# Head loads in smaller pieces, and three bursts of small products per half of a gated recurrence

## The chip, the cores and the metric

The kernel runs on one core of one Trainium2 chip. The metric is the device time of one execution in microseconds (us); the median of several executions is compared. Engines are called PE (TensorE's products; PEld is its weight load), DVE (VectorE), ACT (ScalarE), POOL (GpSimd) and SP (SyncE, which here only issues transfers). PSUM is the memory that PE writes, in banks of 512 f32 per partition; the other tiles lie in SBUF, 128 partitions wide.

## What is computed

One layer of a decoder trunk on 256 tokens of 2048 features, all in f32. Cut to what matters here:

```python
h = rmsnorm(x, norm_mix_g)
u = h @ w_in                     # 2048 -> 12288, split into ten fields
c_g, b_g, xa, za, q, fl, iv, og, ga, gb = split(u)
ya = b_g * causal_dwconv3(c_g * xa, conv_w) * silu(za)
o  = hgrn2_chunked(silu(q), kk(fl), iv, log_f(fl))   # 8 heads of 128
yb = rmsnorm_per_head(o) * silu(og)
m  = sigmoid(ga) * (ya @ w_a_out) + sigmoid(gb) * (yb @ w_b_out)
x  = x + m @ w_o
x  = x + sigmoid(rmsnorm(x) @ w_ple_gate) * (p @ w_ple_proj)
return rmsnorm(x, final_norm_g)
```

The recurrence is a gated linear one: with b the running sum of log_f over the tokens,

```python
a[t, s] = sum_k q[t, k] * exp(b[t, k] - b[s, k]) * kk[s, k]   for s <= t
o[t]    = sum_s a[t, s] * v[s]
```

## The kernel before

**Big products.** Every f32 matrix is split into a high and a low part (`whi`, `wlo` for weights, `xh`, `xl` and the like for activations), and a product is the sum of high x high, high x low and low x high. The main loop at line 940 walks 292 steps. One step holds a chunk of 256 rows and 512 columns of a weight matrix: 2 k tiles x 2 token tiles x 3 parts = 12 products of 128x128 by 128x512 (line 937, in `product`). The groups follow in the order PP (p @ w_ple_proj, one step for each of four column groups), then the fields of w_in for j = 0 and j = 1 (f, q, iv, og, c, xa, za, b; eight steps each), then ga and gb with A and B, then O and PG. Weights come through `load` on SP's queue in tiles called `raw`, and `split` (line 113) makes `whi` on ACT (line 124) and `wlo` on DVE (line 125), three steps ahead of PE, in four buffers. p lies in `praw` and is split by `put_p` on DVE (lines 889 and 890); its split tiles share memory with those of ya and appear in the profile as `yaTh` and `yaTl`.

**The head.** `praw` is loaded in one transfer on SP (line 154). The first step's weights, 128 partitions x 1024, come in two transfers of 128 x 512 by `load_first(0, ...)` (line 106): columns 0 to 511, which are k tile 0, on ACT's queue and the rest on SP's. The second step's weights follow on SP, then small parameters, weights and x by turns. Meanwhile ten products of a zeroed tile (`WARM`, line 816) run on PE. At step 0 the first k tile's products come in the order high x high, low x high (of the activation), high x low.

**Epilogues.** Each group's results are worked on by a generator. `advance` lets each active generator go on to its next `yield` once a step, so that work is spread over steps beside the big products; `step` puts what a generator issues behind the newest split on ACT and DVE. The Tile framework orders the instructions of an engine and sets the semaphores.

**The recurrence.** `hgrn(j)` (line 351) handles four heads and 256 tokens (two blocks of 128) for each half j. Scores inside a block are made in levels B = 128, 64, 32, 16, 8, 4: a pair of tokens belongs to the level at which they lie in the two halves of one stretch of B tokens. `level(B)` (line 424) makes factors exp(+-(b - reference)) on DVE, POOL and ACT and multiplies them into kT and qT, giving a tile X; `products` (line 385) multiplies X's key part by its query part in small tiles (32 or 64 columns) into a PSUM bank; `keep` (line 394) copies the wanted entries under an integer mask into `both` (line 396, in pieces of 32 or 64 partitions). Pairs of neighbouring tokens (B = 2) are done with kT and qT scaled by `f` and `rf` (lines 488 to 501). The cross block between the two blocks of 128 tokens has its own X (line 481) and product (line 512). Two operations split `both` into the scores `a` of the two blocks (line 502), because the second block runs backwards. f32 products of this kind are two records each in the profile.

Before the change PE gets five bursts for each half: levels 128 and 64; 32 and 16; 8 and 4 (line 389, each level into a bank of its own); the cross block with the pairs (lines 512 and 389); and the scores times the values v (lines 529 to 531). Ahead of the last one DVE copies the cross block to `aoff` (line 522) and keeps the pairs by eight masked copies (line 524, recorded at 396).

**The tail.** `last_norm(t)` (line 756) scales the last result by a per-token factor r, in pieces on DVE and ACT, and stores each piece. It is called for t = 0 beside PE's last products, and for t = 1 at the very end.

Of the kernel before, what the change touches and what calls it, by code (L numbers as in the profile page):

```python
# [11 lines left out]
AF = mybir.ActivationFunctionType  # L12
ALU = mybir.AluOpType
PSUM = bass.MemoryType.PSUM

P = 128
T = 256
# [6 lines left out]
CW = 512  # L24
PLE = 256
EPS = 1e-6
WARM = 10
LB_FLOOR = 1e-30
LB_MAX = 1.0 - 1e-6
SCAN = 64  # L30
LEVELS = [128, 64, 32, 16, 8, 4]
# [13 lines left out]
def hybrid_kernel(ctx, tc, xT, x, pT, prm, gfin, masks, w_in, w_a, w_b, w_o, w_pg, w_pp, out):  # L45
    nc = tc.nc
# [35 lines left out]
    def bank(tag):  # L82
        return ps.tile([P, CW], F32, tag=tag, bufs=4, name=nm(tag))
# [22 lines left out]
    def load_first(pos, queues):  # L106

        w, g, c = stream[pos]
        n = 2 * CW // len(queues)
        for i, eng in enumerate(queues):  # L110
            eng.dma_start(out=load(pos)[:, pos % 2, i * n : (i + 1) * n], in_=w[g, :, c, i * n : (i + 1) * n])
# [239 lines left out]
    def hgrn(j):  # L351
# [33 lines left out]
        def products(bk, key, query, B):  # L385

            for h in range(4):
                for r, c in quarters(B):
                    nc.tensor.matmul(  # L389
                        heads(bk)[r, h, c], key(h)[:, r], query(h)[:, c], start=True, stop=True,  # L390
                        tile_position=(0, r.start),
                    )

        def keep(dst, mask, src, B):
            for r, c in quarters(B):
                nc.vector.copy_predicated(  # L396
                    out=dst[r, :, c], data=src[r, :, c],
                    mask=mask_t[r, mask : mask + 1, c].to_broadcast([r.stop - r.start, 4, c.stop - c.start]),
                )

        def halves(ap, B):
            r = ap.rearrange("p (n two h) -> p n two h", two=2, h=B // 2)
# [21 lines left out]
        def level(B):  # L424

            n, h = 1024 // B, B // 2
            e = t4()
            bl, br = halves(b, B)
            el, er = halves(e, B)
            if B > SCAN:  # L430
                nc.scalar.activation(out=el, in_=halves(y, B)[0], func=AF.Exp, scale=-1.0)
                nc.scalar.activation(out=er, in_=br, func=AF.Exp)
            else:
                ref = bl[:, :, h - 1 : h].to_broadcast([P, n, h])
                nc.vector.tensor_tensor(out=el, in0=bl, in1=ref, op=ALU.subtract)
# [9 lines left out]
            in1=tot.rearrange("p (n o) -> p n o", o=1).to_broadcast([P, 16, SCAN]), op=ALU.subtract,  # L445
        )
        yield
        Xs = [level(LEVELS[0])]
        yield
        yield  # L450
        Xs.append(level(LEVELS[1]))
        yield
        yield
        yield

        for i in range(0, len(LEVELS), 2):
            bks = [bank("s") for _ in range(2)]
            for n, X in enumerate(Xs):
                products(bks[n], lambda h: X[:, 0, h, :], lambda h: X[:, 1, h, :], LEVELS[i + n])
            more = i + 2 < len(LEVELS)  # L460
            Xs = [level(LEVELS[i + 2])] if more else []
            yield
            yield
            for n, bk in enumerate(bks):
                keep(both, i + n, heads(bk), LEVELS[i + n])
            if more:
                Xs.append(level(LEVELS[i + 3]))
                yield
                yield
                yield  # L470

        e = t4()
        el, er = halves(e, P)
# [2 lines left out]
            out=el, in0=yl,  # L476
# [4 lines left out]
        X = new_X()  # L481
# [25 lines left out]
        yield  # L507
        bo = bank("s")
        for h in range(4):
            for r in range(2):  # L510
                rows = slice(r * 64, (r + 1) * 64)
                nc.tensor.matmul(
                    heads(bo)[rows, h, :], X[:, 0, h, rows], X[:, 1, h, :], start=True, stop=True,
                    tile_position=(0, r * 64),
                )
# [6 lines left out]
        nc.vector.tensor_copy(out=aoff.rearrange("p h t -> p (h t)"), in_=bo)  # L522
# [233 lines left out]
    def last_norm(t):  # L756

        xs, r, tot = state["x"], sc(1, "r3", 2), state["tot3", t]
        nc.vector.tensor_tensor(out=tot, in0=tot, in1=state["ss3"][:, t * 6 + 4 : t * 6 + 5], op=ALU.add)
        nc.gpsimd.tensor_tensor(out=r, in0=tot, in1=mhalf[:, :1], op=ALU.pow)  # L760
        n = CW // 2

        for eng, q0, q1, queue in (
            (nc.vector, 4, 5, nc.sync), (nc.vector, 5, 6, nc.sync), (nc.scalar, 0, 2, nc.sync),
            (nc.vector, 6, 8, nc.sync), (nc.scalar, 2, 4, nc.scalar),
        ):
            s = slice(q0 * n, q1 * n)
            d = xs[:, t, s]
            if q0 >= 6:
# [3 lines left out]
            elif eng is nc.scalar:  # L773
                nc.scalar.activation(out=d, in_=d, func=AF.Identity, scale=r)
            else:
                nc.vector.tensor_scalar(out=d, in0=d, scalar1=r, scalar2=None, op0=ALU.mult)
            queue.dma_start(out=out[:, t, s], in_=d)

    def ep_last(t, halves):

# [335 lines left out]
```

## Time and profile before

| | |
|---|---|
| median of 3 executions | 831.42 us (831.42 to 831.85) |
| the profiled execution's own time | 831.84 us |
| its span, first to last instruction | 830.1 us |
| instructions in the span | 10589 |
| granted PE clock, mean | 0.996 |
| moved by DMA | 187.25 MB, mean 226 GB/s |

The profile shows one execution. Times in its rows are counted from the span's start. A row of a timeline gives start, length, engine, line, operation and tiles (out<-in), the number of merged instructions (x), and in brackets the idle time of the engine before it and what ended it. A row of a group gives busy us and mean ns of one, then idle time before it. The chain is the sequence of work that ended last, followed back from the last instruction. PE's products are pipelined: their recorded lengths overlap, and the pace is read from their starts.

### The profile page before, as it was taken

What the parts mean: (1) busy time and instruction counts of PE and PEld (TensorE: products, weight loads), DVE (VectorE), ACT (ScalarE), POOL (GpSimd) and SP (SyncE); (2) the same over time, 40 slices, a digit from 0 to 9 for tenths busy, and PEclk for the clock granted to TensorE, in tenths of its full rate; (3) what the DMA queues carried; (4) which work ended last, traced back from release to release, by engine and by line L of the source; (5) the groups of instructions that cost most, each with busy time, mean ns of one, the idle gap of its engine ahead of it and who ended that gap; (6) DMA issues with size and microseconds to landing.
All of it is one profiled execution on the core that took longest, in us unless ns stands there. A gap on an engine that the chain in (4) does not pass through costs nothing.

```text
span 830.1 us, 10589 instructions
## 1 busy us (share of the span) xinstructions
PE 816.9 (98%) x4122; PEld 674.3 (81%) x4122; DVE 538.3 (65%) x662; ACT 430.9 (52%) x553; POOL 84.8 (10%) x74
## 2 busy tenths in 40 slices
PE   9999999999999999999999999999999999999995
PEld 6888888878888888878888888888888888888885
DVE  6746678896866588896745545545645656679633
ACT  7666565446564465455544443443444455566522
POOL 1000035110000054100001001000100000001210
PEclk9999999999999999999999999999999999999998
DMA  9969655647876554657655755755655787987702
GB/s 341 372 256 340 222 193 197 204 153 219 277 235 232 203 203 152 204 192 241 227 203 172 254 189 196 253 203 191 231 191 198 253 281 246 330 304 269 293 0 103
DMA packets 40947, 187.25 MB, mean 226 GB/s; under 512 B 4672, under 2 KB 14400, under 8 KB 22720
## 3 DMA queue, kind: packets, MB, share of 16 engines
q1 hardware_dynamic: 40464, 185.78, 64.7%
q10 hardware_dynamic: 432, 0.79, 0.3%
q8 instruction: 32, 0.52, 0.3%
q14 instruction: 19, 0.16, 0.1%
HBM read 172.92 MB, written 13.63 MB: 225 GB/s over the span
## 4 chain that ended last, share of the span: by engine, by line
PE 93%; DVE 3%; issue 2%; ACT 1%; POOLq 0%; POOL 0%; DVEq 0%
PE g L937 91%; DVE wlo L125 1%; PE s L389 1%; PE s L937 1%; PE s L817 1%; DVE t L264 0%; PE s L531 0%; PE s L529 0%; DVE a L396 0%; ACT whi L124 0%; DVE both L396 0%; DVE X L483 0%; PE s L530 0%; DVE t L492 0%; DVE t L494 0%
## 5 line engine op out<-in xcount | busy, mean ns | idle before, releaser
L125 DVE TENSOR_TENSOR wlo<-raw,whi 128x1024 fp32r<-128x1024 f32 (+1 forms) x293 | 360.4, 1235 | 251.8 <-ACT whi L124 250.8
L124 ACT ACTIVATE whi<-raw 128x1024 fp32r<-128x1024 f32 (+1 forms) x293 | 307.6, 1056 | 323.6 <-PE g L937 279.4
L937 PE MATMUL g<-whi,xh 128*128 128x512 f32 (+1 forms) x912 | 352.0, 387 | 0.0
L937 PE MATMUL g<-whi,xl 128*128 128x512 f32 (+1 forms) x912 | 351.8, 386 | 0.0
L937 PE MATMUL g<-wlo,xh 128*128 128x512 f32 (+1 forms) x912 | 351.7, 386 | 0.0
L937 PEld LDWEIGHTS g<-whi,xh 128*128 128x128 f32 x912 | 171.3, 188 | 34.6
L937 PEld LDWEIGHTS g<-whi,xl 128*128 128x128 f32 x912 | 171.3, 188 | 34.3
L937 PEld LDWEIGHTS g<-wlo,xh 128*128 128x128 f32 x912 | 171.4, 188 | 33.9
L937 PE MATMUL g<-whi,mh 128*128 128x512 f32 x128 | 49.8, 390 | 0.0
L937 PE MATMUL g<-wlo,mh 128*128 128x512 f32 x128 | 49.7, 389 | 0.0
L937 PE MATMUL g<-whi,ml 128*128 128x512 f32 x128 | 49.6, 390 | 0.0
L659 POOL TENSOR_TENSOR t<-ga,gb 128x512 f32<-128x512 f32 x6 | 10.6, 1786 | 195.8 <-DVE gb L654 195.8
L937 PE MATMUL g<-whi,yaTh 128*128 128x512 f32 x72 | 28.3, 399 | 0.0
L937 PEld LDWEIGHTS g<-whi,mh 128*128 128x128 f32 x128 | 24.0, 188 | 5.3 <-ACT mh L665 0.3
L937 PE MATMUL g<-whi,yaTl 128*128 128x512 f32 x72 | 28.3, 396 | 0.0
L937 PEld LDWEIGHTS g<-whi,ml 128*128 128x128 f32 x128 | 23.9, 188 | 5.1 <-DVE ml L666 0.2
L937 PEld LDWEIGHTS g<-wlo,mh 128*128 128x128 f32 x128 | 24.0, 188 | 5.0
L937 PE MATMUL g<-wlo,yaTh 128*128 128x512 f32 x72 | 27.9, 390 | 0.0
L436 POOL TENSOR_TENSOR t<-b 128x512 f32<-128x512 f32 x10 | 18.9, 1890 | 67.0 <-DVE b L319 38.7
L937 PE MATMUL g<-whi,ybTh 128*128 128x512 f32 x64 | 24.9, 389 | 0.0
L937 PE MATMUL g<-whi,ybTl 128*128 128x512 f32 x64 | 24.9, 389 | 0.0
L937 PE MATMUL g<-wlo,ybTh 128*128 128x512 f32 x64 | 24.9, 389 | 0.0
(154 smaller groups left out, 522.4 us busy)
## 6 DMA issues: line engine op xcount, KB each, us to landing
raw<-in_w_in SPq DMA_DIRECT2D x93, 1024.0 KB, 5.0
raw<-in_w_o SPq DMA_DIRECT2D x16, 1024.0 KB, 5.5
raw<-in_w_pg SPq DMA_DIRECT2D x16, 1024.0 KB, 5.8
turn<-t SPq DMA_DIRECT2D x72, 128.0 KB, 2.7
t<-turn SPq DMA_DIRECT2D x18, 512.0 KB, 4.9
raw<-in_w_a SPq DMA_DIRECT2D x8, 1024.0 KB, 5.0
raw<-in_w_b SPq DMA_DIRECT2D x8, 1024.0 KB, 5.0
raw<-in_w_in SPq DMA_DIRECT2D x6, 512.0 KB, 8.3
```

The lines of the kernel that those rows point to most:

```text
L124: a = nc.scalar.activation(out=hi[:, s], in_=src[:, s], func=AF.Copy)
L125: v = nc.vector.tensor_tensor(out=lo[:, s], in0=src[:, s], in1=hi[:, s].bitcast(F32), op=ALU.subtract)
L389: nc.tensor.matmul(heads(bk)[r, h, c], key(h)[:, r], query(h)[:, c], start=True, stop=True, tile_position=(0, r.start),)
L436: nc.gpsimd.tensor_tensor(out=er, in0=br, in1=ref, op=ALU.subtract)
L659: (nc.vector if j == 3 else nc.gpsimd).tensor_tensor(out=spread(m, t), in0=blocks(ga[:, s]), in1=blocks(gb[:, s]), op=ALU.add)
L817: nc.tensor.matmul(wb, warm[:, :P], warm, start=True, stop=True)
L937: nc.tensor.matmul(psum, a, b, start=first and n == 0, stop=last and n == 2)
```

## The change

Four edits stand in the diff.

1. The head: p comes in two transfers (one per k tile) on SP. The first step's weights come, for each k tile, as partitions 0 to 63 on ACT's queue and 64 to 127 on SP's. Six warm-up products instead of ten.
2. The recurrence: the levels 32, 16, 8 and 4 are made first and multiplied in one burst into one bank (each level's 32-wide results at column 32 i of each head), and kept by four masked copies of a whole bank, whose source is repeated along the columns. The levels 128 and 64 are made afterwards and multiplied together with the cross block and the pairs, all in tiles of 32 columns: levels 128, 64 and the first block's pairs share a bank. They are kept by three whole-bank copies under combined masks, which DVE makes once at j = 0. `aoff` is copied by ACT, and one more `yield` stands between these copies and the last burst. Counting `yield`s from the recurrence's start, the bursts stand at 6, 11, 16, 22 and 25 before, at 11, 20 and 24 after.
3. Cross-block products in four tiles of 32 columns instead of two of 64.
4. The tail: `last_norm` uses four pieces of 512 columns instead of two of 256 and three of 512.

```diff
-WARM = 10
+WARM = 6
...
-    nc.sync.dma_start(out=praw.rearrange("p (k t) -> p k t", k=2), in_=pT)
-    load_first(0, (nc.scalar, nc.sync))
+    w0 = load(0)
+    for k in range(2):
+        s = slice(k * CW, (k + 1) * CW)
+        nc.sync.dma_start(out=praw[:, k * T : (k + 1) * T], in_=pT[:, k, :])
+        for eng, part in ((nc.scalar, slice(0, 64)), (nc.sync, slice(64, P))):
+            eng.dma_start(out=w0[part, 0, s], in_=w_pp[0, part, 0, s])
...
         def quarters(B):
-            n = max(B // 2, 32)
-            for r in range(P // n):
-                c = r ^ 1 if B >= 64 else r
-                yield slice(r * n, (r + 1) * n), slice(c * n, (c + 1) * n)
+            for r in range(0, P, 32):
+                c = {128: (r // 64 ^ 1) * 64, 64: r ^ 32}.get(B, r)
+                n = max(B // 2, 32)
+                yield slice(r, r + 32), slice(c, c + n)
...
-        def keep(dst, mask, src, B):
-            for r, c in quarters(B):
+        def keep(dst, mask, src, at=None):
+            if at is None:
                 nc.vector.copy_predicated(
-                    out=dst[r, :, c], data=src[r, :, c],
-                    mask=mask_t[r, mask : mask + 1, c].to_broadcast([r.stop - r.start, 4, c.stop - c.start]),
+                    out=dst, data=src, mask=mask_t[:, mask : mask + 1, :].to_broadcast([P, 4, P])
                 )
+                return
+            n = P // 32
+            nc.vector.copy_predicated(
+                out=dst.rearrange("p h (n c) -> p h n c", n=n),
+                data=src[:, :, at : at + 32].rearrange("p h (n c) -> p h n c", n=1).to_broadcast([P, 4, n, 32]),
+                mask=mask_t[:, mask : mask + 1, :].rearrange("p h (n c) -> p h n c", n=n).to_broadcast([P, 4, n, 32]),
+            )
...
-        Xs = [level(LEVELS[0])]
-        yield
-        yield
-        Xs.append(level(LEVELS[1]))
-        yield
-        yield
-        yield
-        for i in range(0, len(LEVELS), 2):
-            bks = [bank("s") for _ in range(2)]
-            for n, X in enumerate(Xs):
-                products(bks[n], lambda h: X[:, 0, h, :], lambda h: X[:, 1, h, :], LEVELS[i + n])
-            more = i + 2 < len(LEVELS)
-            Xs = [level(LEVELS[i + 2])] if more else []
+        if j == 0:
+            m = lambda i: mask_t[:, i, :]
+            for out, a0, a1, op in ((0, 0, 1, ALU.max), (1, 0, 7, ALU.mult), (0, 0, 6, ALU.mult), (0, 0, 8, ALU.max)):
+                nc.vector.tensor_tensor(out=m(out), in0=m(a0), in1=m(a1), op=op)
+        Xs = []
+        for i in range(2, len(LEVELS)):
+            Xs.append(level(LEVELS[i]))
             yield
             yield
-            for n, bk in enumerate(bks):
-                keep(both, i + n, heads(bk), LEVELS[i + n])
-            if more:
-                Xs.append(level(LEVELS[i + 3]))
+            if i % 2:
                 yield
-                yield
-                yield
+        bk = bank("s")
+        for i, X in enumerate(Xs):
+            products(bk, lambda h: X[:, 0, h, :], lambda h: X[:, 1, h, :], LEVELS[2 + i], 32 * i)
+        Xs = [level(LEVELS[0])]
+        yield
+        yield
+        for i in range(4):
+            keep(both, 2 + i, heads(bk), 32 * i)
+        Xs.append(level(LEVELS[1]))
+        yield
+        yield
+        yield
...
         bk = [bank("s") for _ in range(2)]
+        for i, X in enumerate(Xs):
+            products(bk[0], lambda h: X[:, 0, h, :], lambda h: X[:, 1, h, :], LEVELS[i])
         for blk in range(2):
             kk, qq = (z.rearrange("p (h k t) -> p h k t", h=4, k=2)[:, :, blk, :] for z in (kT, qT))
-            products(bk[blk], lambda h: kk[:, h, :], lambda h: qq[:, h, :], 2)
-        yield
-        yield
-        nc.vector.tensor_copy(out=aoff.rearrange("p h t -> p (h t)"), in_=bo)
-        for blk in range(2):
-            keep(a[:, blk], len(LEVELS) + 2 + blk, heads(bk[blk]), 2)
+            products(bk[blk], lambda h: kk[:, h, :], lambda h: qq[:, h, :], 2, 0 if blk else None)
+        yield
+        yield
+        nc.scalar.activation(out=aoff.rearrange("p h t -> p (h t)"), in_=bo, func=AF.Copy)
+        keep(a[:, 0], 0, heads(bk[0]))
+        keep(a[:, 1], 1, heads(bk[0]))
+        keep(a[:, 1], len(LEVELS) + 3, heads(bk[1]), 0)
+        yield
         yield
...
-        for eng, q0, q1, queue in (
-            (nc.vector, 4, 5, nc.sync), (nc.vector, 5, 6, nc.sync), (nc.scalar, 0, 2, nc.sync),
-            (nc.vector, 6, 8, nc.sync), (nc.scalar, 2, 4, nc.scalar),
-        ):
+        for q in (2, 0, 3, 1):
```

More of the change, by code (lines that the diff above doesn't have):

```diff
@@ L509, in hgrn @@
         for h in range(4):
[L510 to L511 removed]
+            for r in range(0, P, 32):
                 nc.tensor.matmul(
[L513 to L514 removed]
+                    heads(bo)[r : r + 32, h, :], X[:, 0, h, r : r + 32], X[:, 1, h, :], start=True, stop=True,
+                    tile_position=(0, r),
                 )
         bk = [bank("s") for _ in range(2)]
+        for i, X in enumerate(Xs):
+            products(bk[0], lambda h: X[:, 0, h, :], lambda h: X[:, 1, h, :], LEVELS[i])
         for blk in range(2):
             kk, qq = (z.rearrange("p (h k t) -> p h k t", h=4, k=2)[:, :, blk, :] for z in (kT, qT))
[L519 removed]
+            products(bk[blk], lambda h: kk[:, h, :], lambda h: qq[:, h, :], 2, 0 if blk else None)
         yield
         yield
[L522 to L524 removed]
+        nc.scalar.activation(out=aoff.rearrange("p h t -> p (h t)"), in_=bo, func=AF.Copy)
[3 more added lines that the diff above has]
+        yield
         yield
@@ L760, in last_norm @@
         nc.gpsimd.tensor_tensor(out=r, in0=tot, in1=mhalf[:, :1], op=ALU.pow)
-        n = CW // 2
-        for eng, q0, q1, queue in (
-            (nc.vector, 4, 5, nc.sync), (nc.vector, 5, 6, nc.sync), (nc.scalar, 0, 2, nc.sync),
-            (nc.vector, 6, 8, nc.sync), (nc.scalar, 2, 4, nc.scalar),
-        ):
-            s = slice(q0 * n, q1 * n)
-            d = xs[:, t, s]
-            if q0 >= 6:
+        for q in (2, 0, 3, 1):
+            s = slice(q * CW, (q + 1) * CW)
+            d = xs[:, t, s]
+            if q < 2:
+                nc.scalar.activation(out=d, in_=d, func=AF.Identity, scale=r)
+            elif q == 2:
+                nc.vector.tensor_scalar(out=d, in0=d, scalar1=r, scalar2=None, op0=ALU.mult)
+            else:
                 nc.vector.scalar_tensor_tensor(
@@ L772, in last_norm @@
                 )
[L773 to L777, printed above, removed]
+            (nc.scalar if q == 1 else nc.sync).dma_start(out=out[:, t, s], in_=d)
     def ep_last(t, halves):
```

6 lines of the change are left out of this document (3 added, 3 removed).

## The prediction

> **What bounds the kernel now.** I read the page first: the busy times, the busy row of TensorE (PE), the shares of the chain.
>
> ```profile
> PE 816.9 (98%) x4122; PEld 674.3 (81%) x4122; DVE 538.3 (65%) x662; ACT 430.9 (52%) x553; POOL 84.8 (10%) x74
> PE   9999999999999999999999999999999999999995
> PE 93%; DVE 3%; issue 2%; ACT 1%; POOLq 0%; POOL 0%; DVEq 0%
> ```
>
> PE is the bound from the first microseconds to the last slice. So an edit can gain only where PE does something other than its big products at their own pace: the head, the small products of the recurrence, the tail. The list of the chain's pieces in order of time shows the second of these, here for the first half (j = 0):
>
> ```profile
> 17.36 106.08 PE g L937 x468
> 123.44 1.00 PE s L389 x48
> 124.44 13.81 PE g L937 x60
> 138.25 0.69 PE s L389 x50
> 138.94 13.85 PE g L937 x60
> ...
> 170.05 1.02 PE s L512 x16
> 171.07 0.69 PE s L389 x50
> ```
>
> A big product takes 106.08 / 468 = 0.227 us, so one step of the main loop (12 products) takes 2.72 us. Sixty products would take 13.60, but the pieces between bursts take 13.81: each burst costs 0.21 us of switching beside its own time. The first four bursts thus cost 1.00 + 0.21 = 1.21, 0.90, 0.90 (the third, at 152.79, has the piece of the second) and 1.02 + 0.69 + 0.21 = 1.92 us. The fifth, which applies the scores to the values, stands in PE's timeline, and the waits of PE name what holds it:
>
> ```profile
> 180.44 0.39 PE L937 MATMUL g<-whi,xl 128*128 128x512 f32 x1
> 182.13 0.46 PE L529 MATMUL s<-v,a 128*128 128x128 f32 x2 [1.30 <-DVE a L396]
> ...
> 185.10 0.48 PE L937 MATMUL g<-whi,xh 128*128 128x512 f32 x1
> 185.42 0.40 PE L937 MATMUL g<-wlo,xh 128*128 128x512 f32 x1
> ```
> ```profile
> PE s L529 <- DVE a L396: 2.6, 2, 1.3
> ```
> ```profile
>   PEld s L531: 0.4, 2
> ```
>
> From the last big product before it to the second after it pass 185.42 - 180.44 = 4.98 us, 4.53 more than two products. PE stood 1.3 us for the masked copies of VectorE (DVE), which end just ahead of it; the second half does the same (2 waits, 2.6 us), and the view of line 396 adds a short second wait in each (0.4 us in two). One half's five bursts cost 1.21 + 0.90 + 0.90 + 1.92 + 4.53 = 9.46 us.
>
> **The bursts after the change.** Counted in steps of the recurrence, the bursts stand at 6, 11, 16, 22, 25 before and at 11, 20, 24 after. The first new burst has the levels 32 to 4: 128 records of 32x32 instead of two bursts of 64. The second has the cross block (32 records instead of 16, each half as wide), levels 128 and 64 (64 records) and the pairs (64, as before). The third is the old fifth. Paces come from narrow looks at PE:
>
> ```profile
> 123.37 0.69 PE L389 MATMUL s<-X 128*64 128x64 f32 x16
> 123.99 0.45 PE L389 MATMUL s<-X 128*32 128x32 f32 x31
> 169.98 1.09 PE L512 MATMUL s<-X 128*64 128x128 f32 x16
> ```
>
> A record lasts about 0.22, 0.20 and 0.27 us at the end of these rows, so starts follow each other by (0.45 - 0.20) / 30 = 8.4 ns for 32x32, (0.69 - 0.22) / 15 = 31 ns for 64x64 and (1.09 - 0.27) / 15 = 55 ns for the cross block. Two 64-wide records run beside each other; I take it that four 32-wide ones do in the same time, as the 8.4 ns suggest. What a 0.69 piece has beyond 64 x 8.4 ns = 0.54 is 0.15 of run-in. First new burst: 0.21 + 0.15 + 128 x 8.4 ns = 1.44. Second: 0.21 + 0.15 + cross block 0.87 + level 128 0.50 + level 64 0.27 + pairs 0.54 = 2.54. Third without a wait: from 182.13 to 185.42 less one product 3.06, with 0.10 of entry and without the second, short wait 2.96. Sum 6.94 against 9.46: **2.5 us less in each half, 5.0 in all**. Of this 1.57 a half is the wait, 0.95 the two switches and the shared run-in. Bounds: charging the full 0.69 and 1.00 pieces and 1.02 for the cross block to the new bursts makes them 0.5 a half dearer (gain 4.0); lower pieces for the now gapless 32-wide stream give 5.6.
>
> **Why the wait goes.** DVE makes the masked copies in small pieces now and in whole banks afterwards:
>
> ```profile
> L396 DVE COPY_PREDICATED both<-mask_t,s 32x128 f32<-32x128 int32 x40 | 12.0, 299 | 0.8
> ...
> L502 DVE COPY_PREDICATED a<-mask_t,both 128x512 f32<-128x512 int32 x4 | 3.0, 762 | 0.0
> L522 DVE COPY aoff<-s 128x512 f32<-128x512 f32 x2 | 1.4, 683 | 0.0
> ```
>
> Ahead of the last burst stand 8 x 0.30 + 0.68 = 3.1 us on DVE now; afterwards three copies of 0.76 = 2.3, the 0.68 is ACT's, and one more step (2.72 us) lies between them and PE. Against a wait of 1.3 + 0.2 that leaves some 2 us, and the copies stand two steps further from the product with `za` at line 264. The four copies for levels 32 to 4 (3.0 us) replace 16 of 0.30 and nothing on PE asks for them before the last burst. The masks are combined once by four operations on 128 elements (at most 0.30 each, the row above, as bounds nothing to 1.2), long before their use, beside PE's products. ACT's copy waits for a burst two steps old; behind it queue only the splits of weights, three steps ahead of PE, so it costs nothing unless ACT (52% busy) falls more than that behind. The tiles of levels 128 and 64 reuse those of 32 and 16 and are written once the first burst is done, eight steps before they are read.
>
> One place has no slack now: the pairs' products need `kT` scaled by line 500.
>
> ```profile
> 158.72 2.55 DVE L396 COPY_PREDICATED both<-mask_t,s 32x128 f32<-32x128 int32 x8
> ...
> 170.66 0.42 DVE L500 TENSOR_TENSOR kT<-kT,t 128x256 f32<-128x256 f32 x1
> ```
> ```profile
> 171.00 0.76 PE L389 MATMUL s<-qT,kT 128*32 128x32 f32 x64
> ```
>
> Line 500 ends at 171.08 while PE starts those products at 171.00. Afterwards the 2.55 us of copies, which stand straight ahead of that part on DVE, lie three steps earlier, while the product with `c` (line 272, 1.29 for two) comes close; I count some 1.5 us of slack. This is where a loss could sit.
>
> **The head.**
>
> ```profile
> 1.19 4.45 PE L817 MATMUL s<-warm 128*128 128x512 bf16 x10 [1.19 <-DVE warm L813]
> 5.27 1.22 PE L937 MATMUL g<-whi,yaTh 128*128 128x512 f32 x2
> ...
> 7.15 0.65 PE L937 MATMUL g<-wlo,yaTh 128*128 128x512 f32 x2
> ...
> 9.03 0.63 PE L937 MATMUL g<-whi,yaTh 128*128 128x512 f32 x2
> ```
> ```profile
> 0.73 0.42 ACTq L111 DMA_DIRECT2D raw<-in_w_pp  x1
> ...
> 4.59 1.30 ACT L124 ACTIVATE whi<-raw 128x512 fp32r<-128x512 f32 x2 [1.91 <-DMA raw<-in_w_pp]
> 6.57 1.06 ACT L124 ACTIVATE whi<-raw 128x1024 fp32r<-128x1024 f32 x1 [0.68 <-DMA raw<-in_w_pp]
> ```
> ```profile
> 7.66 1.23 DVE L125 TENSOR_TENSOR wlo<-raw,whi 128x1024 fp32r<-128x1024 f32 x1 [0.78 <-ACT whi L124]
> ```
> ```profile
> turn<-t SPq DMA_DIRECT2D x72, 128.0 KB, 2.7
> ...
> raw<-in_w_pp ACTq DMA_DIRECT2D x1, 256.0 KB, 3.8
> t<-in_pT SPq DMA_DIRECT2D x1, 256.0 KB, 3.6
> ```
>
> Ten warm-up products in 4.45 us, the last 0.64 long, follow each other by 0.42 us: half the later pace. The tenth ends its turn at 5.43, so the first real product, ready at 5.27, counts from there. Now 256 KB of weights and 256 KB of `p` must land before it; afterwards 128 KB of each come first, but half of the weights as SP's second issue, 0.43 later. A 128 KB transfer took 2.7, which from 1.17 gives 3.9; the old time is 4.53. I take 4.3, as the queues share engines. With 0.63 on ACT the first product stands near 5.0, 0.43 earlier, worth 0.43 x (0.227 / 0.42) = 0.2 us at the later pace. More than 0.6 can't be had: the second step's `wlo` ends at 8.89 behind a transfer that lands at 6.57, and PE takes it after the two products from 9.03, at about 9.5. Two more SP issues (0.42 each) put every later load's issue 0.85 back; the second step's weights, issued at 1.64 and landed at 6.5, wait for bytes rather than for the issue, so I take nothing; without that cover the head would lose up to 0.5. ACT's extra issue delays its table load by 0.4, hidden before 4.3. **Head: -0.2**, bounds -0.4 (a landing at 3.9) and +0.5, without what the clock may do.
>
> The Trainium skill ("DMA: Bandwidth & Descriptors", "Rules for kernel authors") speaks against this edit: two transfers to disjoint halves of the partitions share all engines, so one over 128 partitions should be used. By it the split gives nothing and the head's term is 0 instead of -0.2; the trace has no load by halves of the partitions.
>
> **The tail** (not in the change's name, but in the diff) joins two pieces of 256 on DVE.
>
> ```profile
> 823.52 0.62 DVE L776 TENSOR_SCALAR xs<-xs,r 128x256 f32<-128x256 f32 x2 [0.67 <-POOL r L760]
> 823.90 2.06 SPq L777 DMA_DIRECT2D out<-xs  x4
> ```
>
> The first store is issued about 0.27 later, the last of three SP issues up to 0.45 earlier, and the same 1 MB follows. I take 0, bounds -0.45 and +0.3. The same edit at t = 0 lies beside PE's last products.
>
> **Sum.** The profiled execution took 831.84 us (span 830.1 and 1.7 around it), 0.4 above the median of 831.42. 831.84 - 5.0 - 0.2 = 826.6, and set against the median **826.2 us**.
>
> **Rivals.**
>
> *The clock comes later* (36%). The pace doubled between 7.15 and 7.40, after 6.0 us in which PE never paused. With six warm-up products PE stops at 1.19 + 6 x 0.42 = 3.7 and stands some 1.3 us. If the 6.0 us have to be unbroken, full pace comes at 5.0 + 6.0 = 11.0 instead of 7.2: 3.8 us at half pace, which lose 3.8 x (1 - 0.227 / 0.42) = 1.8. Time 828.0. For it: nothing else in the trace tells what starts the clock. Against it: once granted, it outlived 2.2 us without work.
>
> ```profile
> 820.49 0.28 PE L937 MATMUL g<-whi,xl 128*128 128x256 f32 x1
> ...
> 822.90:823.10 0.20, 0.00 (x0) 0.00 (x0) 0.00 (x0) 0.00 (x0) 0.17 (x1) 0.69 0.00 0
> ```
>
> PE ended at 820.77, and the granted clock falls to one half inside this last window (mean 0.69). So a pause of 1.3 us may well not count, which is why I forecast no loss, narrowly. The Trainium skill ("TensorE: Matmul & The Clock Gate", Part 1) has the clock granted after a busy window of about 3.4 us on a free-running grid. By that grid the next chance after 7.2 is 10.6, a loss of 1.6; whether a window with such a pause counts as busy, no row shows.
>
> *The wait for the masked copies stays* (9%): DVE is busy without a break around it, and another transpose or split in between would use the slack. Gain 5.0 - 3.1: 829.3.
>
> *The change doesn't pack as it says* (4%): if four 32-wide records of the cross block and level 128 don't run beside each other, they cost 32 x 55 ns and 32 x 31 ns instead of half of that, 1.4 us a half: 829.0. Against it: 8.4 ns a record in the 32x32 rows.
>
> *Slower* (4%): DVE reaches line 500 too late and PE stands at the second burst. The place has no slack now and by my count 1.5 us then. To end 0.2% slower, at 833.1, PE has to lose 833.1 - 826.2 = 6.9 us, 3.45 a half. It decides from where DVE comes 1.5 + 3.45 = 5 us later than counted, that is four copies from PSUM of 2.0 us instead of 0.76. Against it: a piece of 128 elements from PSUM takes 0.30 and one of 512 between tiles 0.76, so PSUM shows no such price.
>
> **Chances.** Forecast 47%, later clock 36, wait stays 9, not packed 4, slower 4. The range has the first two with the bounds of the bursts (1.0 dearer, 0.6 cheaper) and the head: 825.2 to 828.6. Faster or slower by 0.2% is 1.7 us, about what a measurement can tell from no change: the cases at 829.0 and 829.3 are faster too unless the clock is late as well, so faster 0.91, same 0.05, slower 0.04.
>
> **What would show it.** Bursts: three pieces a half, near 1.2, 2.3 and 2.8 us without their switches, and no row of waits of PE on the masked copies. Head: the first product near 5.0, and two products 0.23 apart first at about 7.2 (forecast) or about 11 (rival). Tail: three SP stores, the end as far behind the last product as now. I'd be wrong if PE stands ahead of the second burst, or if the head's loads land later than 4.6.

## The result and the profile after

The changed kernel takes **827.74 us** (median of 4 runs, 827.30 to 827.81), the kernel before 831.52 beside it: ratio 0.9953, 95% interval 0.9935 to 0.9970. The forecast was 826.2, its range 825.2 to 828.6. The profiled execution took 827.30 us, its span 825.2 (before 831.84 and 830.1). So 3.8 us came out of the medians instead of 5.2, and the question is which term of the sum is short of 1.5 us.

The page of after, engines and the shares of the chain:

```profile
PE 812.7 (98%) x4182; PEld 673.1 (82%) x4182; DVE 533.3 (65%) x616; ACT 431.9 (52%) x555; POOL 86.8 (11%) x74
...
PE 96%; issue 1%; DMA 1%; DVE 0%; ACT 0%; SPq 0%; POOLq 0%; POOL 0%
```

VectorE's 3% of the chain is gone, and DMA and SP's queue, which were not on it, have come in. The chain's pieces in order of time (start, length, what) show where:

```profile
0.74 0.39 SPq L157
1.18 0.55 SPq L159
1.78 0.57 SPq L157
2.40 0.47 SPq L159
2.91 5.21 DMA raw<-in_w_pp
8.15 1.07 ACT whi L124
9.24 1.24 DVE wlo L125
10.52 2.57 PE g L949 x10
...
18.53 119.68 PE g L949 x528
138.21 1.29 PE s L393 x96
139.50 24.71 PE g L949 x108
164.21 1.01 PE s L524 x32
165.22 1.34 PE s L393 x108
166.56 11.13 PE g L949 x48
177.69 0.22 PE s L546 x2
...
180.36 138.74 PE g L949 x612
```

(L157 loads `p`, L159 the pieces of the first step's weights; the load that starts at 2.91 is the second step's. L949 is the big product, L393 and L524 are the first and second burst, L546 begins the third.)

Two things are to be seen. The recurrence has become three short pieces in a half with only big products between them. And the head, which before was a chain of products, is now one of SP's issues, a load, its two splits and then products: the piece after the first two groups of output starts at 18.53 instead of 17.36. The time of the 49th big product (here and below the start of its piece in the chain) is **1.17 us later**, where the prediction had it 0.2 earlier.

The waits of PE in after (total, times, longest):

```profile
PE g L949 <- ACT whi L124: 1.5, 1, 1.5
...
PE g L949 <- DVE wlo L125: 1.0, 2, 0.5
```

The 2.6 us behind the masked copies have left the list; 1.5 and 1.0 us behind the splits of the first weights have joined it.

### The profile page after: what moved, and what is told of

Read it like the earlier page. It is cut to its first block, busy times and chain, and to the rows that moved or that the text cites. A ratio compares the mean times of both kernels' runs of the same rounds, so it can differ in the third digit from the quotient of the medians.

```text
span 825.2 us, 10662 instructions
## 1 busy us (share of the span) xinstructions
PE 812.7 (98%) x4182; PEld 673.1 (82%) x4182; DVE 533.3 (65%) x616; ACT 431.9 (52%) x555; POOL 86.8 (11%) x74
## 4 chain that ended last, share of the span: by engine, by line
PE 96%; issue 1%; DMA 1%; DVE 0%; ACT 0%; SPq 0%; POOLq 0%; POOL 0%
PE g L949 94%; PE s L949 1%; PE s L393 1%; DMA raw<-in_w_pp 1%; PE s L524 0%; PE s L548 0%; PE s L547 0%; PE s L546 0%; ACT xs L782 0%; DVE wlo L125 0%; ACT whi L124 0%; SPq L159 0%; SPq L157 0%; DVE t L752 0%; DVE t L756 0%
## 5 line engine op out<-in xcount | busy, mean ns | idle before, releaser
L125 DVE TENSOR_TENSOR wlo<-raw,whi 128x1024 fp32r<-128x1024 f32 (+1 forms) x293 | 365.4, 1252 | 251.1 <-ACT whi L124 250.1
L949 PE MATMUL g<-wlo,xh 128*128 128x512 f32 (+1 forms) x912 | 351.9, 386 | 0.0
L949 PE MATMUL g<-whi,xl 128*128 128x512 f32 (+1 forms) x912 | 351.8, 386 | 0.0
L949 PE MATMUL g<-whi,xh 128*128 128x512 f32 (+1 forms) x912 | 351.6, 386 | 0.0
L949 PEld LDWEIGHTS g<-wlo,xh 128*128 128x128 f32 x912 | 171.5, 188 | 34.2
L949 PEld LDWEIGHTS g<-whi,xl 128*128 128x128 f32 x912 | 171.4, 188 | 34.2
L949 PEld LDWEIGHTS g<-whi,xh 128*128 128x128 f32 x912 | 171.4, 188 | 34.1
L949 PE MATMUL g<-whi,mh 128*128 128x512 f32 x128 | 49.8, 390 | 0.0
L949 PE MATMUL g<-wlo,mh 128*128 128x512 f32 x128 | 49.7, 390 | 0.0
L949 PE MATMUL g<-whi,ml 128*128 128x512 f32 x128 | 49.6, 390 | 0.0
L949 PE MATMUL g<-whi,yaTh 128*128 128x512 f32 x72 | 27.8, 393 | 1.5 <-ACT whi L124 1.5
L949 PE MATMUL g<-wlo,yaTh 128*128 128x512 f32 x72 | 28.2, 394 | 1.0 <-DVE wlo L125 1.0
L949 PEld LDWEIGHTS g<-whi,mh 128*128 128x128 f32 x128 | 24.0, 188 | 5.2 <-ACT mh L682 0.3
L949 PEld LDWEIGHTS g<-whi,ml 128*128 128x128 f32 x128 | 24.0, 188 | 5.1 <-DVE ml L683 0.2
L949 PEld LDWEIGHTS g<-wlo,mh 128*128 128x128 f32 x128 | 24.1, 188 | 5.0
L949 PE MATMUL g<-whi,yaTl 128*128 128x512 f32 x72 | 27.9, 390 | 0.0
L949 PE MATMUL g<-wlo,ybTh 128*128 128x512 f32 x64 | 24.9, 390 | 0.0
L949 PE MATMUL g<-whi,ybTh 128*128 128x512 f32 x64 | 24.9, 389 | 0.0
L949 PE MATMUL g<-whi,ybTl 128*128 128x512 f32 x64 | 24.9, 389 | 0.0
```

The lines of the kernel that those rows point to most:

```text
L125: v = nc.vector.tensor_tensor(out=lo[:, s], in0=src[:, s], in1=hi[:, s].bitcast(F32), op=ALU.subtract)
L949: nc.tensor.matmul(psum, a, b, start=first and n == 0, stop=last and n == 2)
```

## The experiments

Each group of four ran beside the kernel before on one chip: its median was 831.70 us beside e1 to e4, 831.38 beside e5 to e8, 831.73 beside e9 to e12. "Old loads" are those of before: `p` whole, the first weights by columns over both queues. Line numbers are those of each kernel, a few off from one to the next.

### e1: the change without its head

```diff
-WARM = 6
+WARM = 10
...
-    w0 = load(0)
-    for k in range(2):
-        ...
+    nc.sync.dma_start(out=praw.rearrange("p (k t) -> p k t", k=2), in_=pT)
+    load_first(0, (nc.scalar, nc.sync))
```

> The changed kernel with the head of before: p in one transfer, the first step's weights by columns, ten warm-up products. In the profiled execution of the changed kernel PE took the second step's low weights at 10.52 us, before the change at about 9.5, and its first 48 products ended at 18.53 instead of 17.36. Theory: the smaller loads put the second step's weights 1.2 us later, whatever the clock does; then this kernel takes 827.7 - 1.2 = 826.5 us. Rival (an accident of that one execution, slow packets at 4.2 to 5.2 us): 827.5 to 827.9, the same as the changed kernel. Second rival (six warm-up products delay the clock): also about 826.2 to 826.7, but then the next kernel but two, with ten products and the new loads, is as fast.

Measured: 826.64 us (826.21 to 827.38), ratio 0.9941 [0.9929, 0.9954], 1.1 us less than the whole change. Its chain has the 49th product at

```profile
17.42 119.68 PE g L945 x528
```

The head of the change costs time; the rest gains 5.1 us.

### e2: the new head alone

The other way round: before, with the loads and the six warm-up products of after (the same lines as in e1, swapped).

> The kernel before with the new head alone (loads in smaller pieces, six warm-up products). Theory that the smaller loads come later: 831.5 + 1.2 = 832.7 us. Prediction's step (head gains 0.2): 831.3. Accident: 831.5.

Measured: 832.75 us (832.27 to 833.66), ratio 1.0015 [1.0006, 1.0024]: 1.05 us slower than before. The first row is of the chain, the next fence of PE's waits:

```profile
19.00 106.08 PE g L941 x468
```
```profile
PE s L533 <- DVE a L400: 2.6, 2, 1.3
PE g L941 <- ACT whi L124: 1.6, 1, 1.6
```

The wait for the masked copies stands as it did, and the new wait for the first weights stands beside it. So the two halves of the change add up, within the scatter: -5.1 and +1.05 against -3.8 measured.

### e3: the recurrence alone

The change with the old loads, ten warm-up products and the old tail (`last_norm` of before).

> The kernel before with the recurrence's edits alone (three bursts per half, combined masks, cross block on ACT); head and tail as before. Between the first 48 products and the last product the profiled executions differ by 5.6 us, against 5.0 predicted. Theory: 831.5 - 5.5 = 826.0 us; if the switches cost nothing and only the wait for the masked copies went, 828.4. The distance to the kernel with the old head (which has the new tail too) is the tail: 0.4 us by the two profiles, 0 by the prediction.

Measured: 826.76 us (826.35 to 827.74), ratio 0.9942 [0.9930, 0.9955]. That is 4.9 us for the recurrence, and 0.1 between the old tail and the new one (e1), less than the runs scatter.

### e4: the change with ten warm-up products

```diff
-WARM = 6
+WARM = 10
```

> The changed kernel with ten warm-up products instead of six, new loads kept. Theory of the late loads: PE waits for data until 5.4 us in any case and ten products end at 5.5, so 827.6 to 827.9 as the changed kernel. Rival, the pause after six products delays the clock in most executions: 826.3 to 827.0, with the mean clock at 0.997 in each run instead of 0.994 to 0.997.

Measured: 827.89 us (827.19 to 828.23), ratio 0.9954 [0.9941, 0.9966]: as the change itself. The chain:

```profile
18.64 11.56 PE g L949 x51
```

With four more warm-up products the 49th product is no earlier (18.64 against 18.53). In this execution the number of warm-up products isn't what holds the new head. The medians agree, but by themselves they couldn't show it: ten warm-up products cost half a microsecond elsewhere, as the part on all runs says.

### e5: only one more step for the masked copies

```diff
             keep(a[:, blk], len(LEVELS) + 2 + blk, heads(bk[blk]), 2)
+        yield
         yield
```

> The kernel before with one more yield between the masked copies and the last burst, nothing else. Theory: the wait of PE for the masked copies (2.6 + 0.4 us in two bursts) goes and the switches stay, so 831.7 - 3.0 = 828.7 us and no row of waits on the copies. Rival: DVE is so full around it that the copies come later too, part of the wait stays: 829.5 to 831.5.

Measured: 828.30 us (828.08 to 828.66), ratio 0.9964 [0.9950, 0.9977], 3.1 us less than before with one line. PE's waits in e5:

```profile
PE g L938 <- ACT whi L124: 0.5, 1, 0.5
```

The row of the masked copies is gone. This is 1.54 us a half, and the prediction had 1.57 of its 2.5 for the wait. What e3 gains beyond it, 4.94 - 3.08 = 1.9, is the shape of the bursts (predicted 0.95 a half, 1.9). It is rather more in the change itself, since e3 loses half a microsecond that the change doesn't (the part on all runs).

### e6: e1 without the additional step

```diff
         keep(a[:, 1], len(LEVELS) + 3, heads(bk[1]), 0)
         yield
-        yield
```

> The changed kernel with the head of before and without the extra yield, so that the last burst comes one step after the three whole-bank copies. Theory: the three copies (2.3 us instead of 3.1, aoff on ACT) end in time by some 0.9 us, so 826.6 as with the yield. Rival: the yield is what takes the wait away; then PE waits for the copies again, up to 1.3 us in each half, 827.5 to 829.2.

Measured: 826.71 us (826.39 to 826.85), ratio 0.9943 [0.9930, 0.9955]. DVE's timeline (the last masked copy ahead of the third burst) and PE's (the burst's first products):

```profile
172.63 0.73 DVE L402 COPY_PREDICATED a<-mask_t,s 128x512 f32<-128x512 int32 x1
```
```profile
174.07 0.38 PE L541 MATMUL s<-v,a 128*128 128x128 f32 x2
```

The copy ends at 173.36, PE comes at 174.07. The whole-bank copies, with the cross block on ACT, take the wait away without the step, with 0.7 us to spare; so does the step alone (e5). The change has both.

### e7 and e8: the smaller loads one at a time

e7 is the change with `p` by k tiles, but with each k tile's weights over all 128 partitions; e8 has `p` whole and the weights by halves of the partitions.

```diff
     w0 = load(0)
+    for k, eng in enumerate((nc.scalar, nc.sync)):
         s = slice(k * CW, (k + 1) * CW)
         nc.sync.dma_start(out=praw[:, k * T : (k + 1) * T], in_=pT[:, k, :])
+        eng.dma_start(out=w0[:, 0, s], in_=w_pp[0, :, 0, s])
```

> The changed kernel with p still by k tiles and the first weights again by columns over all 128 partitions (ACT the first half, SP the second); six warm-up products. SP has one issue fewer ahead of the second step's weights. If the halves of the partitions make the loads late: about 826.7 us and the second step's weights landed by 7.0 us. If many small transfers do: about 827.2, landed near 7.6. If p by k tiles does: 827.7, near 8.2.

```diff
     w0 = load(0)
+    nc.sync.dma_start(out=praw.rearrange("p (k t) -> p k t", k=2), in_=pT)
     for k in range(2):
         s = slice(k * CW, (k + 1) * CW)
-        nc.sync.dma_start(out=praw[:, k * T : (k + 1) * T], in_=pT[:, k, :])
         for eng, part in ((nc.scalar, slice(0, 64)), (nc.sync, slice(64, P))):
             eng.dma_start(out=w0[part, 0, s], in_=w_pp[0, part, 0, s])
```

> The changed kernel with p in one transfer again and the first weights by halves of the partitions over two queues; six warm-up products. The reverse of the other: 827.7 us and landed near 8.2 if the halves make the loads late, about 827.2 if many small transfers do, 826.7 and 7.0 if p by k tiles does.

Measured: e7 827.11 us (826.45 to 827.92), ratio 0.9949 [0.9937, 0.9962]; e8 827.59 us (826.57 to 828.42), ratio 0.9954 [0.9942, 0.9967]. Against e6's 826.71, with the old loads in the same group, that is 0.4 us more for `p` and 0.9 for the halves. Taken as medians neither is clear: the interval of each holds e6's ratio, and e6 has ten warm-up products where these have six. e7 comes nearest to its second case (many small transfers), e8 to its first (the halves), so the two don't settle which part is at fault. The chain of e7:

```profile
2.11 5.64 DMA raw<-in_w_pp
...
18.16 12.01 PE g L948 x53
```

With `p` split, the second step's weights are SP's fourth issue, at 2.11 instead of 1.64, behind the same bytes as with the old loads. They landed at 7.75 (e6: 6.79). That gave the next four runs their question: is the load late because it is *issued* late, or because more pieces *use the engines* worse?

### e9: the second step's weights on ACT's queue

```diff
-    load_first(1, (nc.sync,))
+    load_first(1, (nc.scalar,))
```

> The changed kernel, with the second step's weights issued from ACT's queue behind the two weight pieces there, and no longer from SP's behind five transfers. Theory A, the head is late because its second load is issued late (SP has five issues ahead of it): the load goes out about 1.2 us earlier, lands near 6.9 instead of 8.1 us, the 49th big product ends near 17.4, and the time is 826.6 to 826.9. Theory B, the small pieces use the DMA engines badly whatever the order of the issues: the load still lands near 8 us, the 49th product ends near 18.4, and the time is 827.5 to 827.9.

Measured: 829.07 us (827.84 to 830.37), ratio 0.9966 [0.9952, 0.9979]: worse than either theory had it. The chain of e9:

```profile
2.40 6.10 DMA raw<-in_w_pp
...
9.26 6.75 PE g L949 x18
...
21.45 8.61 PE g L949 x38
```

The edit did something else than was meant. The 512 KB, now issued at 1.98, went ahead of the last 128 KB of the *first* step's weights, which SP issues at 2.40 as before; they landed at 8.5 instead of 6.8, and PE stood for them. In PE's timeline of e9 the products then follow each other slowly for long:

```profile
13.14 0.63 PE L949 MATMUL g<-whi,yaTl 128*128 128x512 f32 x1
13.56 0.62 PE L949 MATMUL g<-whi,yaTh 128*128 128x512 f32 x1
```

Products 0.42 us apart up to 13.56: full pace came after that; whether the pause put it off, one run doesn't show. The run doesn't tell the two theories apart; it shows that the order of the loads matters, and what the rival of the late clock looks like when it does come true.

### e10: e1 with the second step's weights on ACT's queue

The edit of e9, in e1. Here only 256 KB stand ahead of it on ACT's queue and nothing of the first step is issued later than 1.2 us.

> The loads of before with ten warm-up products, the recurrence of after; only the second step's weights are issued from ACT's queue, behind one transfer instead of behind two on SP's. Theory A (the issue sets the landing): the load goes out about 0.5 us earlier and lands near 6.4, the 49th product ends 0.3 to 0.5 earlier, near 16.8, and the time is 826.2 to 826.4. Theory B (the bytes ahead of it set the landing): it lands at 6.0 to 6.9 as with the loads of before, the 49th product at 17.2, and the time is 826.5 to 826.8.

Measured: 826.47 us (826.11 to 827.21), ratio 0.9938 [0.9925, 0.9950]. The issue stood at 1.18 instead of 1.64; the 49th product at

```profile
17.48 119.68 PE g L945 x528
```

The load landed at 6.9, as in e1 with the issue at 1.64, and the product is no earlier. An issue before 1.64 gains nothing: up to there it isn't the issue that sets the landing, as theory B has it. In time it is the least of all kernels here, but its interval holds e1's ratio, so the two aren't told apart.

### e11: e1 with six warm-up products

```diff
-WARM = 10
+WARM = 6
```

> The loads of before, the recurrence of after, and six warm-up products instead of ten. If the clock of the head is what the time hangs on, full pace comes at about 9.5 us in some executions and the time is up to 1.0 us longer than with ten, 827.2 to 827.7. If the head waits for its data and not for the clock, it is within 0.3 us of the same kernel with ten: 826.4 to 826.9.

Measured: 826.93 us (826.71 to 827.60), ratio 0.9944 [0.9932, 0.9957], 0.5 above e10 in the same group, at the upper end of what was expected if the head waits for data alone. PE's timeline and the chain:

```profile
7.53 1.06 PE L945 MATMUL g<-wlo,yaTh 128*128 128x512 f32 x2
8.38 0.74 PE L945 MATMUL g<-whi,yaTh 128*128 128x512 f32 x2
8.96 0.40 PE L945 MATMUL g<-wlo,yaTh 128*128 128x512 f32 x1
```
```profile
18.24 11.79 PE g L945 x52
```

Two products from 7.53 to 8.38, two from 8.38 to 8.96, then 0.23 each: the pace doubles near 8.5 in this execution, and the 49th product is 0.76 later than in e10. So with the old loads, which come in time, the later clock costs that execution 0.76 us at the 49th product. In the medians it isn't shown: the interval of e11 holds the ratios of e10 and e1.

### e12: one small transfer more ahead of the second step's weights

```diff
-    load_first(1, (nc.sync,))
     prm_t = const.tile([P, PRM_N], F32, name="prm_t")
     nc.sync.dma_start(out=prm_t, in_=prm)
+    load_first(1, (nc.sync,))
```

> The loads of before with ten warm-up products, the recurrence of after; the small parameter load (36 KB) is issued on SP ahead of the second step's weights instead of behind them. One more issue of a small transfer ahead of that load, with nearly no bytes. Theory A (the issue sets the landing): it goes out 0.25 to 0.5 us later and lands near 7.3, the 49th product ends near 17.6 and the time is 826.9 to 827.2. Theory B (the bytes set it): 36 KB of the 384 KB ahead of it cost about 0.1 us, and the time is 826.6 to 826.8.

Measured: 827.21 us (826.85 to 827.69), ratio 0.9947 [0.9934, 0.9959], 0.7 above e10 in the same group. Its chain:

```profile
2.11 5.69 DMA raw<-in_w_pp
...
18.22 11.79 PE g L945 x52
```

The loads are the old ones, whole; 36 KB ahead of this one push its issue from 1.64 to 2.11, and the 49th product from 17.42 to 18.22, as far as the splitting of `p` did in e7. The intervals of e12 and e10 overlap, but the spans of their five executions don't: 825.1 to 825.7 here, 824.3 to 824.7 in e10. So behind 1.64 **a later issue** does make the load late, as theory A says, but not as it says: the issue moved by 0.47 us and the landing, 7.80 against e1's 6.93, by 0.87 (theory A had 7.3). e7, with the same issue and without the 36 KB ahead, lands at 7.75, so it isn't these bytes.

### What the runs give together

| kernel | second step's weights issued, us | landed, us | GB/s from 4 to 6 us | 49th big product, us | median against before, us |
|---|---|---|---|---|---|
| e10 | 1.18 (ACT) | 6.9 | 415 | 17.48 | -5.26 |
| e1 | 1.64 | 6.9 | 408 | 17.42 | -5.06 |
| e6 (one `yield` less) | 1.65 | 6.8 | 415 | 17.23 | -4.67 |
| e11 (six warm-ups) | 1.64 | 6.9 | 407 | 18.24 | -4.80 |
| e12 | 2.11 | 7.8 | 335 | 18.22 | -4.52 |
| e7 (six warm-ups) | 2.11 | 7.8 | 329 | 18.16 | -4.27 |
| e8 (six warm-ups) | 2.41 | 8.0 | 247 | 18.55 | -3.79 |
| e4 | 2.90 | 8.2 | 200 | 18.64 | -3.81 |
| after (six warm-ups) | 2.91 | 8.1 | 208 | 18.53 | -3.78 |

e1 and e6, whose heads are alike, differ by 0.4 in the last column, so smaller steps there say nothing. The 49th product is late for two reasons that have to be kept apart. In e12, e7, e4 and after the chain runs through the late load. In e11 it doesn't, and PE works at half pace at first; nor does it in e8:

```profile
1.19 3.60 DMA raw<-in_w_pp
...
5.56 7.55 PE g L949 x24
```

Here the first 24 products alone take 7.55 us (6.28 before): they follow each other by 0.42 us up to 9.14, and the second step's `wlo` is ready at 10.38, 0.3 before PE takes it. So e8's 18.55 is the later clock's as much as the load's.

The number of warm-up products does something more. From the 49th product to the start of the last one the profiles of the five kernels with the new recurrence and six warm-ups (after, e7, e8, e9, e11) show 797.5 to 797.7 us, those of the six with ten 798.1 to 798.3. In these six alone PE stands 0.2 to 0.4 us after the sixth big product behind the second burst of the first half. e4 has it as

```profile
168.69 0.50 PE L949 MATMUL g<-whi,xh 128*128 128x512 f32 x1 [0.36 <-issue]
```

where "issue" means that the profile shows nothing that PE waits for. Its cause stays open. But wherever kernels with six and with ten are compared, half a microsecond isn't the head's.

The fourth column comes from the view by windows, whose last two columns are the mean busy share of the DMA engines and what they moved. The windows from 4 to 6 us of before, after and e12:

```profile
4.00:6.00 2.00, 2.00 (x6) 0.93 (x5) 1.58 (x5) 1.26 (x2) 0.30 (x1) 1.00 1.06 403
```
```profile
4.00:6.00 2.00, 0.58 (x3) 0.49 (x4) 0.00 (x0) 0.63 (x1) 0.52 (x1) 1.00 1.04 208
```
```profile
4.00:6.00 2.00, 2.00 (x7) 0.96 (x6) 1.59 (x5) 1.25 (x2) 0.53 (x1) 1.00 1.03 335
```

The engines are shown as busy in all three, and move half as much in after. The packet records say how: of the 4 KB packets that start in this window, which are those of the second step's weights, 8 of 48 in after took 0.5 to 1.5 us, 1.0 in the mean, and 8 of 102 in e12 0.5 to 1.0; nearly all of before's 139 took 0.16 and none over 0.4. Such packets stand in the profiles of e2, e4, e7 and e9 too, but not in e8, where none of 65 took over 0.5 us and the rate is low all the same. What stretches them stays open. So does the share of the halves: in e8 and after they come on top of a later issue, and no run separates the two.

## Why the prediction was right or wrong

**The bursts: right, 0.6 us too cautious.** The prediction's way of counting, on the chain of after: first burst 1.29 and 24.71 - 108 x 0.2267 = 0.23 of switching, 1.52 (predicted 1.44); second 1.01 + 1.34 + 11.13 - 48 x 0.2267 = 2.60 (2.54); third from 177.69 to 180.36 = 2.67 (2.96). Sum 6.79 against 6.94. The old bursts were counted too low: from the 49th product to the start of the last one pass 820.49 - 17.36 = 803.13 us before and 816.06 - 18.53 = 797.53 after, 5.60 less instead of 5.0, so five old bursts cost 6.79 + 2.80 = 9.6 a half instead of 9.46. In medians the recurrence alone is 4.9 (e3, with the stand of PE that kernels with ten warm-ups have). That four records of 32 columns run beside each other is in PE's timeline of after:

```profile
138.13 1.36 PE L393 MATMUL s<-X 128*32 128x32 f32 x128
164.13 1.08 PE L524 MATMUL s<-X 128*32 128x128 f32 x32
...
165.81 0.75 PE L393 MATMUL s<-qT,kT 128*32 128x32 f32 x64
```

Thirty-two narrow records of the cross block take 1.08, where sixteen of twice the width took 1.09. The rival *not packed* falls.

**The wait: right.** 3.1 us in e5 as in the sum, and the rival *the wait stays* falls in e1, e3, e5 and e6. The place without slack that the rival *slower* needed is not one: DVE's timeline of after has line 513 (500 before) and the last masked copy at

```profile
162.70 0.40 DVE L513 TENSOR_TENSOR kT<-kT,t 128x256 f32<-128x256 f32 x1
...
173.36 0.75 DVE L406 COPY_PREDICATED a<-mask_t,s 128x512 f32<-128x512 int32 x1
```

The first ends 2.7 us ahead of the pairs' products at 165.81 (I counted 1.5), the second 3.6 ahead of the third burst at 177.69 (2).

**The head: wrong, and this is the step that failed.** Of the load of the second step's weights the prediction says that they "wait for bytes rather than for the issue, so I take nothing". That holds for before, and e10 confirms it: half a microsecond earlier gains nothing. But the load stood at the edge. One issue later (e12, e7) it lands 0.8 to 0.9 us later than in e1, and e12 loses 0.5 (against e1) to 0.7 us (against e10). The price given for the case that this cover is gone, up to 0.5, was too low too, for two reasons. The two more issues put it back by 2.91 - 1.64 = 1.27 us instead of 0.85, since SP's issues of the pieces took 0.47 to 0.57 where those of before took 0.42. And nothing between the landing and PE takes up the delay: by the chain above the second step's `whi` starts at 8.15 instead of 6.57, its `wlo` at 9.24 instead of 7.66. That is 1.58 later, of which before had 0.6 to spare; 0.3 of it is more than the issue moved, and goes with the slow packets. The early landing, the term's only gain, was mis-sized as well. ACT's timeline of after, the first split:

```profile
4.73 0.63 ACT L124 ACTIVATE whi<-raw 128x512 fp32r<-128x512 f32 x1 [1.28 <-DMA raw<-in_w_pp]
```

The first pieces land at about 4.7, not 4.3, past the 4.6 that the prediction names as its limit, and PE starts at 5.42 instead of near 5.0. The halves brought nothing: the first split starts at 4.6 to 5.1 in the five kernels that have them, and at 4.6 to 5.1 in the eight with the old loads. In e7, with `p` split and the weights whole, it starts at 4.25 and the first product at 4.93, as forecast; the late second load takes that back. By medians the head's term is +1.05 (e2) to +1.1 (after against e1) where it was put at -0.2 within -0.4 and +0.5.

The Trainium skill ("DMA: Bandwidth & Descriptors", "Rules for kernel authors") spoke against transfers to disjoint halves of the partitions, since they share all engines; by it the term was 0. The runs agree that the halves gain nothing. That the head as a whole loses 1 us comes, in the profile of after, of the later second load.

**The later clock: a real mechanism, but not the loss that the profile of after shows.** 827.74 lies nearer to that rival's 828.0 than to the forecast, and for another reason. That the range holds it is largely luck: its upper part was there for this rival, and the forecast's own bounds end at 826.2 + 1.0 + 0.5 = 827.7. PE's timeline of after:

```profile
1.19 2.74 PE L829 MATMUL s<-warm 128*128 128x512 bf16 x6 [1.19 <-DVE warm L825]
5.42 0.74 PE L949 MATMUL g<-whi,yaTh 128*128 128x512 f32 x2 [1.49 <-ACT whi L124]
6.00 0.63 PE L949 MATMUL g<-whi,yaTl 128*128 128x512 f32 x2
```

After the pause of 1.49 us the first products already follow each other by 0.29 and then 0.23: full pace, before the forecast's 7.2, let alone 11. Then PE stands twice more for data, 1.0 us in all (the row of `wlo` in its waits). And e4, with ten warm-up products, is no faster. But the rival does appear: in four of the six profiles with six warm-ups (e2, e8, e9, e11) full pace came at 8.6 us or later, and in none of the eight with ten. In e11 it cost 0.76 us at the 49th product. In e2 it cost next to nothing, for the second step's `wlo` was ready only at 10.90 and PE took it at 10.95. The other executions of after have no profile, so a share of its loss in them isn't excluded.

**The tail: right at 0.** The last product of after, and SP's three last stores as foretold:

```profile
816.06 0.28 PE L949 MATMUL g<-whi,xl 128*128 128x256 f32 x1
```
```profile
819.60 1.56 SPq L789 DMA_DIRECT2D out<-xs  x3
```

From that product's end to the span's end are 8.9 us (before 9.3); e1 and e3, which differ in the tail alone, have 9.1 and 8.9 and medians 0.1 apart.

**The sum.** The measured terms, -5.60 for the bursts, +1.17 for the head and -0.4 for the tail of these two executions, come to -4.8 us; their spans differ by 4.9. The kernel without the new head, e1 at 826.64 or with e10's edit 826.47, is what the forecast of 826.2 describes.

## What to carry to other kernels

Splitting a first load into smaller pieces is paid for by the load behind it: list every issue that the queue makes ahead of the *next* load that PE will need, and add their measured durations, before the earlier first product is booked. "It waits for bytes" says nothing on how much later it may be issued; a load can sit right on that edge. Try each edit alone, too: four warm-up products more or fewer moved half a microsecond some 165 us later. And a wait with a named releaser (here masked copies in small pieces) is often worth one more step of distance, the cheapest edit of all (3.1 of 5 us here).

## What the runs showed of the hardware

- **DMA engines shown as busy can move half their rate.** From 4 to 6 us the share is 1.03 to 1.06 in before, after and e12, and the rate 403, 208 and 335 GB/s.
- **When full pace comes differs between executions of like kernels.** By the clock records of the traces, which the starts of the products bear out, it came at 3.9 us in e7, 4.5 in after, 8.6 in e11, 9.5 in e8, 9.7 in e2 and 14.0 in e9, all with six warm-up products, and at 4.0 (e4) to 7.2 (before) in the eight with ten. The granted clock of the windows is printed as 1.00 all through, also where products follow each other by 0.42 us, so the starts of the products are the row to read. The Trainium skill ("TensorE: Matmul & The Clock Gate", Part 1) says that the window on which the clock is granted runs freely and doesn't begin with the kernel; the spread of these times agrees with it. Why it came as late as 14.0 in e9 isn't shown.
- **Half pace costs little while data are late.** e2 worked at half pace up to 9.6 us and still came to the second step's `wlo` (10.95) when it was only just ready (10.90). In after, full pace from the first product on didn't help, since PE then stood 1.0 us more for the weights.
